# A decoder layer in split fp32: order of loads, casts and products at four places, and who makes the low parts

## The chip, the core and the metric

The kernel runs on one core of one Trainium2 chip. The metric is the device time of one execution in microseconds (us), median of several runs. The engines are PE (TensorE), DVE (VectorE), ACT (ScalarE), POOL (GpSimd) and SP, whose queue issues nearly all transfers.

## The reference, cut to what matters

One decoder layer on x (1024 tokens, width 1024, fp32), with 256 memory tokens. Three sub-layers, each with an RMS norm ahead and a residual behind:

```python
h = rms_norm(x, norm_mix)
rq, rk, rv, rg, dq, dk, dv = split(h @ w_in)
o_ret  = rms_norm(retention(rotary(rq), rotary(rk), rv)) * silu(rg)
o_diff = rms_norm(diff_attention(norm(dq), norm(dk), dv, lam), diff_subln) * 0.8
x = x + (concat(o_ret, o_diff) * group_scale) @ w_out
k, v = split(rms_norm(mem, norm_mem) @ xkv);  q = norm(rms_norm(x, norm_x) @ xq)
x = x + softmax(q @ norm(k).T / 16) @ v @ xo
h = rms_norm(x, norm_ffn)
x = x + (silu(h @ w_gate) * (h @ w_up)) @ w_down
```

Retention has 8 heads of 64 in chunks of 128 tokens, differential attention 4 heads, cross-attention 4 heads of 256; the FFN is 2816 wide.

## The kernel before, in words

**Split products.** Each fp32 operand of a large product is held as a high part (a cast to fp32r, mostly on ACT) and a low part (the rest, a subtract in `low`, L104, on DVE or POOL). `mm3` (L134) issues three matmuls for each block: high by high, high by low, low by high. `unit` (L121) loads one 128 x 1024 block of a weight into a staging buffer (`raw`, three buffers; some into `t4`, six), casts it and makes its low part on the engine named by `eng`.

**Who sets the order.** PE's instructions keep the order of the program. Those of the other engines and the transfers are ordered at compile time by a scheduler, by program position and by when it expects operands and buffers; `tc.high_priority()` moves a block ahead of it, and `keep_in_program_order` pins single ones. A tile waits for a free buffer of its pool: PSUM has two buffers each of `mm`, `ms` and the two-bank `s2`.

**Start.** `xT` is x transposed, in four pairs (q) of 256 tokens and two halves (j). `load_xT` (L219) loads one and, except for q = 0, multiplies it by the norm's gain on POOL in four pieces; `split_x` (L234) casts and subtracts it; for q = 0 the gain is in both. `token_norm` takes the squares of the token rows on ACT and their inverse roots on DVE. The loop over n (L739) then runs 64 items, eight token blocks of each of eight heads: `gemm` (projection, four items ahead, in four parts), `e1` and `e3` (norm and transpose of keys), `m1`, `m2`, `m3` (scores, transposes, values).

**Memory stage.** The last items run beside `Mem.gemm` (L632): keys and values of the memory tokens for eight column blocks c, 24 matmuls for each of two token blocks t. `Mem.load` loads the two weight units of block c + 2. The finished heads lie in DRAM as `mix_d`; `load_mix` (L693), called at the end of block c, loads one head's rows into a `raw` buffer, and casts and splits it. Four of the six `t4` buffers hold the memory tokens in this stage. The output projection (L827) follows, its four weight units a column half; each token block's norm and transposes (`to_hT`, kept as closures in `mend`) run behind, the last four of them after the projection.

**Cross-attention.** Items n = 4 h + p, head h, token pair p: `xG` query product, `xR` inverse norms, `xS` scores, `xT_` transposes of the weights, `xO` values, `xX` (L997) output product in four parts (two token blocks, two column halves), each added to the residual `xr` on DVE. For the last head, `xX` also takes the FFN's norm of the pair: square on ACT, inverse root and scale on DVE into a tile `xn_f` (two buffers), then `b_sums` (L847) makes four differences of its quarters.

**Border to the FFN.** The FFN's first products use seven forms (1 to 7) of the normed input, a recursion that saves one product in eight. `b_part(p, f)` (L870) transposes form f of pair p on PE, casts the high part on ACT and makes the low part: for pair 0 on DVE; for others a product with minus the identity (`negI`) subtracts the high part in PSUM and ACT casts the rest, one `b_part` later (`b_flush`). `Forms` makes the forms of a weight pair, and `GU` (L1154) runs the products; the first weight is done in two halves, `c0` (pairs 0 and 1) and `c1` (pairs 2 and 3).

**End.** The down projection sums 11 pairs of hidden blocks for each of seven forms (L1332); for the last form the last three pairs are held back and done one output block i after the other, so that `d_out` adds and stores each as it is finished.

## Time and profile before

| | |
|---|---|
| runs of before | 1631.23, 1631.32, 1632.48 us; median 1631.32 |
| the profiled execution's own time | 1633.47 us |
| its span, first to last instruction | 1631.7 us |
| busy share: PE, DVE, ACT, POOL | 95%, 61%, 38%, 19% |
| mean granted clock of PE | 0.985 |
| chain that ended last, by engine | PE 76%, DVE 13%, ACT 4%, DMA 3%, POOL 2% |

The span is that of one profiled execution. Busy time counts an engine's instructions; PE's are pipelined, so that a busy PE need not be at its peak. "Idle before" is time an engine stood before an instruction, with what released it. PEclk is the clock granted to PE, 1.00 being 2.4 GHz and 0.50 being 1.2 GHz. An engine that is not the bottleneck may idle at no cost.

### The profile page before, as it was taken

What the parts mean: (1) busy time and instruction counts of PE and PEld (TensorE: products, weight loads), DVE (VectorE), ACT (ScalarE), POOL (GpSimd) and SP (SyncE); (2) the same over time, 40 slices, a digit from 0 to 9 for tenths busy, and PEclk for the clock granted to TensorE, in tenths of its full rate; (3) what the DMA queues carried; (4) which work ended last, traced back from release to release, by engine and by line L of the source; (5) the groups of instructions that cost most, each with busy time, mean ns of one, the idle gap of its engine ahead of it and who ended that gap; (6) DMA issues with size and microseconds to landing.
All of it is one profiled execution on the core that took longest, in us unless ns stands there. A gap on an engine that the chain in (4) does not pass through costs nothing.

```text
span 1631.7 us, 23450 instructions
## 1 busy us (share of the span) xinstructions
PE 1555.4 (95%) x8797; PEld 1328.1 (81%) x8797; DVE 995.0 (61%) x2494; ACT 626.9 (38%) x1209; POOL 310.8 (19%) x428
## 2 busy tenths in 40 slices
PE   6899999999999889999999979999999999999998
PEld 6778888878888878799999867887888888788886
DVE  6954864964866633755555855666666666555554
ACT  5442443442445531332233454333333333343332
POOL 5423323323303432111112220000000000000000
PEclk9899999999999999999999999999999999999999
DMA  8201011111103552100101222444444444788562
GB/s 287 72 27 50 34 40 40 44 40 39 40 14 134 188 182 91 40 13 29 39 27 39 78 91 67 165 149 148 149 148 149 161 149 162 256 302 260 202 211 78
DMA packets 69233, 180.85 MB, mean 111 GB/s; under 512 B 7424, under 2 KB 12928, under 8 KB 69120
## 3 DMA queue, kind: packets, MB, share of 16 engines
q1 hardware_dynamic: 68112, 178.81, 31.1%
q8 instruction: 69, 1.13, 0.3%
q10 hardware_dynamic: 1008, 0.55, 0.1%
q14 instruction: 44, 0.36, 0.1%
HBM read 135.55 MB, written 43.78 MB: 110 GB/s over the span
## 4 chain that ended last, share of the span: by engine, by line
PE 76%; DVE 13%; ACT 4%; DMA 3%; POOL 2%; issue 1%; SPq 0%; ACTq 0%; DVEq 0%; POOLq 0%
PE x L64 15%; PE g_r L64 8%; PE z L64 7%; PE dx L64 7%; PE dy L64 6%; PE xq L64 5%; PE wo L64 5%; PE xo L64 5%; PE y L64 3%; PE kv L64 3%; PE q L64 2%; PE av L64 2%; DVE nmx L52 2%; DVE dsm L52 1%; PE rsk L64 1%
## 5 line engine op out<-in xcount | busy, mean ns | idle before, releaser
L64 PE MATMUL g_r<-uh_r,xT 128*128 128x512 f32 x512 | 179.3, 408 | 0.0
L52 DVE TENSOR_TENSOR dl<-ds,dh 128x1024 fp32r<-128x1024 f32 x77 | 93.9, 1223 | 93.2 <-PE dx L64 37.4
L52 ACT CAST dh<-ds 128x1024 fp32r<-128x1024 f32 x77 | 80.7, 1055 | 123.8 <-PE dy L64 49.9
L64 PEld LDWEIGHTS g_r<-uh_r,xT 128*128 128x128 f32 x512 | 97.1, 190 | 22.5 <-issue 2.4
L64 PE MATMUL x<-Bh,f 128*128 128x512 f32 (+1 forms) x368 | 113.3, 380 | 1.4 <-DVE G L52 1.4
L52 POOL TENSOR_TENSOR G<-G,U 128x512 f32<-128x512 f32 (+1 forms) x23 | 35.3, 1537 | 408.5 <-DVE U L52 347.5
L64 PE MATMUL kv<-uh_d,xT 128*128 128x256 f32 x512 | 109.6, 297 | 1.2 <-DVE dql L52 1.2
L52 DVE TENSOR_TENSOR f<-s,f 128x512 fp32r<-128x512 f32 x86 | 65.4, 761 | 62.2 <-ACT f L52 62.2
L64 PE MATMUL g_r<-ul_r,xT 128*128 128x512 f32 x256 | 101.1, 395 | 0.0
L52 ACT CAST f<-s 128x512 fp32r<-128x512 f32 x88 | 54.6, 621 | 106.2 <-DVE s L52 105.7
L64 PE MATMUL xq<-hT,uh_xq 128*128 128x256 f32 x512 | 94.3, 286 | 0.0
L64 PE MATMUL xo<-uh_xo,xoT 128*128 128x512 f32 x256 | 89.4, 409 | 3.6 <-DVE xr L52 2.0
L64 PEld LDWEIGHTS kv<-uh_d,xT 128*128 128x128 f32 x512 | 86.0, 195 | 3.7 <-DVE dql L52 1.4
L52 ACT ACTIVATE p<-s,nmx,dsm 128x128 f32<-128x128 f32 (+7 forms) x64 | 53.2, 832 | 87.0 <-DVE nmx L52 86.2
L64 PEld LDWEIGHTS xq<-hT,uh_xq 128*128 128x128 f32 x512 | 80.5, 193 | 0.0
L64 PEld LDWEIGHTS x<-Bh,f 128*128 128x128 f32 x368 | 68.3, 188 | 14.9 <-DVE G L52 1.8
L52 DVE TENSOR_TENSOR G<-x,G 128x512 f32<-128x512 f32 (+1 forms) x69 | 45.6, 661 | 50.2 <-ACT G L52 47.8
L64 PE MATMUL kv<-ul_d,xT 128*128 128x256 f32 x256 | 73.5, 287 | 1.0 <-DVE ul_d L52 1.0
L64 PE MATMUL xq<-hT,ul_xq 128*128 128x256 f32 x256 | 73.1, 286 | 0.0
L52 DVE TENSOR_TENSOR f<-gu,f 128x512 fp32r<-128x512 f32 x61 | 42.0, 689 | 49.6 <-ACT f L52 49.6
L64 PE MATMUL dx<-dh 128*128 128x512 f32 x176 | 68.8, 391 | 1.6 <-DVE res L52 1.6
L64 PE MATMUL x<-Bl,f 128*128 128x512 f32 (+1 forms) x184 | 69.9, 380 | 0.0
(337 smaller groups left out, 4257.0 us busy)
## 6 DMA issues: line engine op xcount, KB each, us to landing
gu<-in_w_dram SPq DMA_DIRECT2D x21, 1024.0 KB, 6.0
ds<-gF_d SPq DMA_DIRECT2D x77, 256.0 KB, 4.0
wd<-in_w_dram SPq DMA_DIRECT2D x22, 512.0 KB, 5.6
wT_d<-wd SPq DMA_DIRECT2D x22, 512.0 KB, 3.0
ds<-wT_d SPq DMA_DIRECT2D x44, 256.0 KB, 4.0
ds<-in_w_dram SPq DMA_DIRECT2D x33, 256.0 KB, 5.1
st_r<-in_w_dram SPq DMA_DIRECT2D x16, 512.0 KB, 3.2
st_kv<-in_w_dram SPq DMA_DIRECT2D x16, 512.0 KB, 3.4
```

Of the source, the lines that this page charges most:

```text
L52: r = f(*args, **kw)
L64: return tc.keep_in_program_order(nc.tensor.matmul(*args, **kw))
```

## The change

Start: pair q = 1 of `xT` takes its gain in `split_x`, like q = 0, and no longer on POOL; the scores of item 0 (`m1`) are issued behind the third quarter of the next projection. Memory stage: all low parts of its weights go to DVE; `load_mix` is called at the start of block c with a `t4` buffer, and the new `split_mix` casts at the end of c; in the output projection units 0 and 2 have DVE for the low part and 1 and 3 POOL, the reverse of before. Cross-attention: the first query product `xG(0)` is issued ahead of the four last transposes rather than after the first of them. Border: `b_sums` of pair 1 goes to POOL, in pieces of 256 columns; low parts of pairs 0 and 1, and of forms 2, 5, 7 and 4 of the others, go to DVE; only items 14 and 15 have high priority in `xX`; the transposes, values and output products of item 15 are issued earlier, and the `b_part` calls of pairs 1 to 3 are spread between the FFN's first products. End: two pairs are held back, not three.

```diff
--- before.py
+++ after.py
@@ -1,4 +1,4 @@
-from contextlib import ExitStack
+from contextlib import ExitStack, nullcontext
 
 import numpy as np
 
@@ -221,7 +221,7 @@
         st = stage(f"xs{q}_{j}")
         xst[q, j] = st.rearrange("p (k t) -> p k t", k=4)
         sp.dma_start(xst[q, j], a["xT"][:, 4 * j:4 * j + 4, 256 * q:256 * q + 256])
-        if q:
+        if q > 1:
             g = bc(gains[:, G_MIX + 4 * j:G_MIX + 4 * j + 4], 256)
             for i in range(4):
                 tc.keep_in_program_order(gp.tensor_tensor(out=xst[q, j][:, i:i + 1], in0=xst[q, j][:, i:i + 1],
@@ -235,7 +235,7 @@
 
         s3 = xst.pop((q, j))
         hv, o = xT[q // 2], 256 * (q % 2)
-        if q:
+        if q > 1:
             hi, lo = (hv[:, 4 * j:4 * j + 4, x, o:o + 256] for x in range(2))
             sc.copy(hi, s3)
             low(ve, lo, s3, hi)
@@ -629,12 +629,13 @@
 
         def load(self, c):
             if c < 8:
-                self.u[c] = [unit(U_KV + 2 * c + i, f"kv{c}_{i}", eng=ve if i else gp, pool=up if i else uqp, pin=c < 1) for i in range(2)]
+                self.u[c] = [unit(U_KV + 2 * c + i, f"kv{c}_{i}", eng=ve, pool=up if i else uqp, pin=c < 1) for i in range(2)]
 
         def gemm(self, c, i):
             t, h = divmod(i, 2)
             if i == 0:
                 self.load(c + 2)
+                load_mix(c)
             if h == 0:
                 self.ps = mm(f"xkv_{c}_{t}")
             ps = self.ps
@@ -650,7 +651,7 @@
                 sc.activation(sq, dst, AF.Square, accum_out=self.ssk[:, 4 * t + c:4 * t + c + 1])
             if t == 0:
                 return
-            load_mix(c)
+            split_mix()
             if c == 3:
                 rsqrt(self.ssk, 8, 1.0 / 256, "kx")
                 for j in range(2):
@@ -690,16 +691,22 @@
 
     kord = [g + (4 if kind == "d" else 0) for kind, g in order]
 
+    mixs = []
+
     def load_mix(i):
-        if i >= len(kord) - 1:
-            return
-        kb = kord[i]
-        st = raw(f"mixs{kb}")
-        sp.dma_start(st, mix_d[kb])
-        for h in range(2):
-            sl = slice(512 * h, 512 * h + 512)
-            sc.copy(mixT[h][:, kb, 0, :], st[:, sl])
-            low(ve, mixT[h][:, kb, 1, :], st[:, sl], mixT[h][:, kb, 0, :])
+        if i < len(kord) - 1:
+            kb = kord[i]
+            st = t4(f"mixs{kb}")
+            sp.dma_start(st, mix_d[kb])
+            mixs.append((kb, st))
+
+    def split_mix():
+        if mixs:
+            kb, st = mixs.pop(0)
+            for h in range(2):
+                sl = slice(512 * h, 512 * h + 512)
+                sc.copy(mixT[h][:, kb, 0, :], st[:, sl])
+                low(ve, mixT[h][:, kb, 1, :], st[:, sl], mixT[h][:, kb, 0, :])
 
     def run_fin(last=False):
         if fins:
@@ -754,7 +761,6 @@
         if n == 0:
             call("e3", 0)
             call("e3", 1)
-            call("m1", n)
             split_x(3, 1)
             call("e1", 3)
             token_norm(3)
@@ -763,6 +769,8 @@
             ws[1] = [load_part(*order[1], i) for i in range(4)]
         drain(pend2)
         gemm(n + LEAD, (2,))
+        if n == 0:
+            call("m1", n)
         run_fin()
         gemm(n + LEAD, (3,))
         drain(pend3)
@@ -825,7 +833,7 @@
             dst[t // 4] = big.tile([P, KB, 2, 512], F32R, tag="A", name=f"{name}{t // 4}")
 
     for c in range(2):
-        u = [unit(U_OUT + 4 * c + i, f"wo{c}_{i}", eng=ve if i % 2 else gp, pool=ntp if c and i < 2 else None)
+        u = [unit(U_OUT + 4 * c + i, f"wo{c}_{i}", eng=gp if i % 2 else ve, pool=ntp if c and i < 2 else None)
              for i in range(4)]
         for t in range(NT):
             ps = mm(f"wo_{c}_{t}")
@@ -848,12 +856,13 @@
 
         ev, od = xns
         xns.clear()
-        eng = gp if p < 1 else ve
+        eng = gp if p < 2 else ve
         T1, T2, T4 = (hfp.tile([P, 512], F32, tag=f"bs{i}", bufs=1, name=f"bs{p}_{i}") for i in (1, 2, 4))
         T3 = od[:, 0:512]
         for dst, l, r in ((T1, od[:, 0:512], ev[:, 0:512]), (T2, od[:, 512:1024], T1), (T4, ev[:, 512:1024], T2),
                           (T3, od[:, 512:1024], od[:, 0:512])):
-            eng.tensor_tensor(out=dst, in0=l, in1=r, op=ALU.subtract)
+            for c in cut4(512) if eng is gp else (slice(0, 512),):
+                eng.tensor_tensor(out=dst[:, c], in0=l[:, c], in1=r[:, c], op=ALU.subtract)
         bsrc[p] = {1: ev[:, 0:512], 2: ev[:, 512:1024], 3: od[:, 512:1024], 5: T1, 6: T2, 7: T3, 4: T4}
 
     def b_tiles(f):
@@ -876,7 +885,7 @@
         lo, hi = (x[:, :, P * p:P * p + P] for x in b_tiles(f))
         sc.copy(hi, p3)
         b_flush()
-        if p == 0:
+        if p < 2 or f in (2, 5, 7, 4):
             low(ve, lo, p3, hi)
             return
 
@@ -1004,14 +1013,15 @@
                       cols(uo[i:i + 1], 0, 1024, 512 * c, 512)) for i in range(2)])
 
             sl = xr[t][:, 512 * c:512 * c + 512]
-            ve.scalar_tensor_tensor(out=sl, in0=ps, scalar=Z[:, e:e + 1], in1=sl, op0=ALU.mult, op1=ALU.add)
+            with tc.high_priority() if n > 13 else nullcontext():
+                ve.scalar_tensor_tensor(out=sl, in0=ps, scalar=Z[:, e:e + 1], in1=sl, op0=ALU.mult, op1=ALU.add)
             if h == 3 and c == 1:
                 sp.dma_start(res_d[t], xr[t])
                 if e == 0:
                     hd["r"] = small(2, "rn2", f"rf{p}")
                 xn = xnp_tile(f"xn_f{t}")
                 xns.append(xn)
-                with tc.high_priority():
+                with tc.high_priority() if n > 13 else nullcontext():
                     r = hd["r"]
                     sc.activation(xn, xr[t], AF.Square, accum_out=r[:, e:e + 1])
                     if p == 3:
@@ -1024,8 +1034,8 @@
                     if e:
                         b_sums(p)
 
+    xG(0)
     mend.pop(0)(mm)
-    xG(0)
     mend.pop(0)(mm)
     head_k(0)
     mend.pop(0)(mm)
@@ -1055,16 +1065,18 @@
     xS(15)
     b_part(0, 5, ms)
     xX(14, (0, 1))
-    b_part(0, 6, mm)
+    b_part(0, 6, ms)
+    with tc.high_priority():
+        xT_(15)
+    xX(14, (2, 3))
     b_part(0, 4, ms)
-    xX(14, (2, 3))
-    for i, f in enumerate((1, 2, 3)):
-        b_part(1, f, (mm, ms)[i % 2])
-    xT_(15)
-    for i, f in enumerate((5, 6, 7, 4)):
-        b_part(1, f, (mm, ms)[i % 2])
-    xO(15)
+    with tc.high_priority():
+        xO(15)
+    b_part(1, 1, ms)
+    b_part(1, 2, ms)
+    xX(15, (0, 1))
     b_flush()
+    xX(15, (2, 3))
 
 
 
@@ -1222,26 +1234,29 @@
     f0.form(1, gp)
     f0.form(2, gp)
     o = GU(0, f0)
+    def b_parts(p, *fs):
+        for f in fs:
+            nb[0] += 1
+            b_part(p, f, (ms, ms, mm)[nb[0] % 3])
+
+    nb = [0]
+    for f, eng in ((5, gp), (6, ve), (3, gp), (7, ve), (4, gp)):
+        f0.form(f, eng)
     o.go(1, c0)
+    b_parts(1, 3, 5)
     o.go(2, c0)
-    for f, eng in ((5, gp), (6, ve), (3, gp)):
-        f0.form(f, eng)
-    xX(15, (0, 1), ms)
-    xX(15, (2, 3), ms)
-    f0.form(7, ve)
-    f0.form(4, gp)
+    b_parts(1, 6, 7)
     o.go(5, c0)
+    b_parts(1, 4)
     o.prod(6, c0)
-    for i, f in enumerate((1, 2, 3)):
-        b_part(2, f, (mm, ms)[i % 2])
+    b_parts(2, 1, 2)
     o.go(3, c0)
-    for i, f in enumerate((5, 6, 7)):
-        b_part(2, f, (ms, mm)[i % 2])
+    b_parts(2, 3, 5)
     o.go(7, c0)
-    b_part(2, 4, mm)
+    b_parts(2, 6, 7)
     o.go(4, c0)
-    for i, f in enumerate((1, 2, 3, 5, 6, 7, 4)):
-        b_part(3, f, (ms, mm)[i % 2])
+    b_parts(2, 4)
+    b_parts(3, 1, 2, 3, 5, 6, 7, 4)
     fn = Forms(1)
     o.go(1, c1)
     b_flush()
@@ -1341,12 +1356,12 @@
             if (f, p) not in du:
                 d_load(f, p, raw if p % 2 else t4)
                 d_cast(f, p)
-            if f != d_order[-1] or p < NP - 3:
+            if f != d_order[-1] or p < NP - 2:
                 for i in range(4):
                     d_prod(f, p, i)
         if f == d_order[-1]:
             for i in range(4):
-                for p in range(NP - 3, NP):
+                for p in range(NP - 2, NP):
                     d_prod(f, p, i)
                 d_out(f, i)
         else:
```

## Rows read from the trace of the kernel before

**Rows 1.** Windows by stage: us, busy PE, PEld, DVE, ACT, POOL; PEclk, DMA, GB/s.

```profile
17.00:60.00 43.00, 31.60 (x212) 29.53 (x211) 37.80 (x174) 26.48 (x56) 29.09 (x41) 0.80 0.56 198
...
500.00:592.00 92.00, 79.20 (x553) 72.14 (x551) 53.62 (x108) 49.02 (x96) 44.17 (x55) 0.93 0.51 181
...
730.00:900.00 170.00, 169.53 (x1176) 157.58 (x1176) 94.74 (x254) 51.51 (x105) 36.91 (x51) 1.00 0.11 38
...
930.00:970.00 40.00, 31.24 (x177) 24.94 (x175) 28.76 (x67) 21.59 (x43) 9.14 (x10) 0.96 0.29 113
970.00:1013.00 43.00, 37.37 (x229) 31.97 (x230) 19.73 (x45) 23.25 (x46) 1.91 (x3) 0.96 0.08 25
```

**Rows 2.** Windows of two of the stretches at half clock, columns as above.

```profile
43.45:53.69 10.24, 6.90 (x33) 6.47 (x33) 10.21 (x58) 3.75 (x8) 5.58 (x8) 0.50 0.30 110
...
685.16:688.57 3.41, 3.41 (x18) 3.41 (x18) 3.10 (x12) 0.86 (x2) 1.28 (x1) 0.50 0.35 129
```

**Rows 3.** Waits of PE over the span: waiting, releaser, us in total, times, longest.

```profile
PE xkv L64 <- ACT vx L52: 7.6, 3, 4.0
...
PE s L64 <- DVE dkT L52: 4.7, 1, 4.7
PE q L64 <- ACT dkv L52: 3.7, 1, 3.7
...
PE tr_x L68 <- DVE xr L52: 2.7, 1, 2.7
```

**Rows 4.** Timeline of the start, engines ACT, POOL and DVE: start, us, what.

```profile
10.02 1.71 ACT L52 ACTIVATE xT<-xs,gains 128x256 fp32r<-128x256 f32 x4 [1.31 <-DMA xs<-in_xT_dram]
...
23.18 1.04 ACT L52 ACTIVATE x<-x 128x1024 f32<-128x1024 f32 x1
...
14.29 12.40 POOL L52 TENSOR_TENSOR xs<-xs,gains 128x256 f32<-128x256 f32 x16 [13.23 <-DMA xs<-in_xT_dram]
...
24.34 0.17 DVE L52 TENSOR_SCALAR rx_x<-rstd 128x2 f32<-128x2 f32 x1 [0.41 <-ACT x L52]
...
47.01 0.34 DVE L52 SCALAR_TENSOR_TENSOR dkT<-dkt,gx,dkT 128x128 fp32r<-128x128 f32 x1
```

**Rows 5.** Groups by form, 500 to 592 us: busy us, mean ns, idle before.

```profile
L52 POOL TENSOR_TENSOR ul_kv<-st_kv,uh_kv 128x256 fp32r<-128x256 f32 x32 | 28.8, 933 | 34.4 <-ACT uh_kv L52 34.4
...
L52 ACT CAST uh_kv<-st_kv 128x1024 fp32r<-128x1024 f32 x16 | 16.5, 1046 | 15.7 <-DMA st_kv<-in_w_dram 15.4 <-PE xkv L64 0.3
...
L52 DVE TENSOR_TENSOR ul_kv<-st_kv,uh_kv 128x1024 fp32r<-128x1024 f32 x8 | 10.3, 1290 | 10.5 <-ACT uh_kv L52 10.4
...
L52 ACT CAST mix<-mixs 128x512 fp32r<-128x512 f32 x14 | 8.1, 620 | 12.1 <-DMA mixs<-mix_d 12.1
```

**Rows 6.** Chain of waits, 500 to 592 us: start, us, what.

```profile
535.70 2.79 PE xkv L64 x24
...
576.66 3.27 DMA mixs<-mix_d
```

**Rows 7.** Windows of two parts of the border, columns as in the first group.

```profile
936.60:942.00 5.40, 1.78 (x8) 1.10 (x7) 5.40 (x9) 0.00 (x0) 0.00 (x0) 1.00 0.09 37
942.00:951.00 9.00, 6.79 (x40) 4.78 (x41) 2.31 (x9) 8.36 (x18) 0.00 (x0) 1.00 0.15 60
```

**Rows 8.** Groups by form, 930 to 1000 us, of ACT and DVE.

```profile
L52 DVE SCALAR_TENSOR_TENSOR xn_f<-xr,rf,g_ffn 128x1024 f32<-128x1024 f32 x6 | 7.5, 1283 | 0.3
...
L52 ACT ACTIVATE xn_f<-xr 128x1024 f32<-128x1024 f32 x4 | 4.3, 1086 | 0.0
L52 DVE TENSOR_TENSOR bs<-xn_f,bs 128x512 f32<-128x512 f32 x6 | 4.1, 684 | 0.0
```

**Rows 9.** Timeline of DVE around the start of a POOL subtract at 507.05.

```profile
506.88 0.16 DVE L52 TENSOR_TENSOR rw_m<-ry_m 128x2 f32<-128x2 f32 x1
...
507.85 0.67 DVE L52 SCALAR_TENSOR_TENSOR ry_m<-rw_m,ry_m 128x2 f32<-128x2 f32 x1
```

**Rows 10.** Chain of waits at the end of the kernel.

```profile
1624.60 0.70 DVE res L52
```

## The prediction

> **What bounds the kernel now.** The page's first part shows TensorE (PE) busy for 95% of the span and VectorE (DVE), the next, for 61%. So I asked for the busy time of each engine in stretches and looked where PE's share falls. In most of the kernel it idles for under 3%; the exceptions [rows 1] are four: 11.4 us of idle in the start, 12.8 us in the stage that multiplies the memory tokens while heads finish, and 8.8 + 5.6 us in the border from cross-attention to the FFN. The fourth is one wait at the border into cross-attention, below. In the same places the granted clock is 0.50, that is 1.2 instead of 2.4 GHz [rows 2]: after an idle of 2 to 5 us PE works at half speed for 3.41, 6.83 or 10.24 us. Besides the two stretches shown, the places that the change touches hold two of 6.83 us, at 23.0 and 558.9, and four of 3.41: at 514.5 and 582.8 (memory stage), 961.6 and 971.9 (border). The PE time inside such a stretch is lost by half. All else in the kernel is PE at work, which the change barely touches. So the question is who ends each wait: the list of PE's waits names them [rows 3], and I read each in the timeline of the engine named.
>
> **Start (17 to 60 us).** PE waits 3.7 us for the copy `dkv`, and that copy stood on ScalarE (ACT) behind the cast of the second token pair and behind two squares of `x`, the second from 23.18 to 24.22 [rows 4]; the cast waited for 8 gain multiplies on GpSimd (POOL). Then PE waits 4.7 us for DVE's last `dkT` part, at 47.01; from 24.34 on DVE is never idle, so that end is set by when DVE could begin. The change gives the gains of that pair to the cast, as for the first: 8 ACT pieces (four took 1.71 us) and 8 DVE pieces of about 0.5 us instead of two of 1.2 to 1.7 us: about +0.5 us for DVE. The first half of the pair has landed when POOL takes it up, at 14.29 [rows 4]; with the second half close behind and 3.4 us of ACT pieces the cast can end near 18 to 19, the squares near 20, where the second now ends at 24.22. DVE begins 3 to 4 us sooner; later pairs' loads do not move, so I take 3. Moving the scores of block 0 behind the next 12 products fills 1.4 us of the second wait (24 took 2.79 us [rows 6]; double that at half clock). **Sum: -4.5.** Bounds: 0, if the later loads set DVE's chain, and -8, two thirds of the idle and of the half-speed loss.
>
> **Memory stage (500 to 592 us).** The chain of waits runs in a ring: a low part on POOL (32 pieces, 28.8 us), a load into the staging buffer that it frees, a cast, PE [rows 5, 6]. ACT stands 15.4 us for weight loads and 12.1 us for `mixs` loads, and PE's next product waits for the evacuation `vx` queued behind such a cast. The change breaks the ring in three places. The `mix` rows get their own buffer and are issued one step ahead of the cast, while PE has 48 products, 5.6 us, against a load of 3.27; this moves seven DMAs on SP's queue past the cast and returns the third staging buffer to the weights. Eight low parts go from POOL, four pieces of 0.93 us each, to DVE, 1.29 us each: DVE +10.3, to 64 of 92 us. And the output weights that are used first get the faster engine. To be won: 12.8 of idle and half of about 11.7 us of work at 1.2 GHz, 18.7 together. I leave 8: 2.1 at the heads' own waits (511 to 523), some 2 of the 4 us at 557 where ACT stands behind a reduce of DVE, 1.7 for one half-speed stretch, 2.2 at the first output weights and elsewhere. **Sum: -10.5.** Bounds: -4, if the new buffer (six, four of them held by the memory tokens) gives no lead and only POOL's part counts, and -15.
>
> **Into cross-attention (681 us).** The transposes need the PSUM buffer whose reader `xr` stands in DVE's queue behind a norm: 2.7 us, then 3.41 us at 0.50, which costs 1.7 [rows 2, 3]. The query product now goes first: 48 products, 5.6 us, inputs ready, so the reader is covered. But two transposes now follow each other on two PSUM buffers, each waiting for a cast and a subtract (1.3 us); I give back 1.4. **Sum: -3**, bounds 0 and -4.4.
>
> **Border (930 to 1013 us).** Two views tell the halves apart [rows 7]. From 936.6 to 942 DVE is busy throughout (norms and sums of the second pair, put first) while PE works 1.8 of 5.4 us; from 942 to 951 ACT is full, casting high and low parts, while DVE stands idle for three quarters. The change: (a) 15 low parts leave PE and ACT for DVE: 15 products of 512 columns less on PE, at 0.23 us twice those of 256 [rows 6], 3.5; ACT -9; DVE +10.3 at 0.68, the time of a sum of that size [rows 8]; (b) the sums of pair 1 go to POOL, DVE -2.7, with work between them and their first use; (c) products stand between the transposes. To be won: 14.4 idle, 3.4 of half speed, 3.5 of products: 21.3. Put back: the norm of a pair needs the two `xn_f` buffers, whose last readers, transposes 3 and 7, now come late. Pair 2: a square of 1.09, some 13 small DVE operations of 0.2 each, a scale of 1.28 [rows 8, 9] are 5.1 us from transpose 7 of pair 1, against 3.6 us of products and a transpose group: 1.5. Pair 3 the same with ten small operations: 4.6 against 3.4, 1.2, and its four sums of 0.68 chained with low parts on one engine, 2. Behind the last attention output 0.7. DVE's added 7.6 us (10.3 - 2.7) come where it is busy 58% of the time: I take 3.6 on the path. Two half-speed stretches stay, 3.4. Together 12.4. **Sum: -9.** Bounds: -2 and -15.
>
> **Last pairs.** Holding two pairs back instead of three leaves the count of products and the last add and store as they are; the waits for that add (0.70 us, [rows 10]) stay, one for each buffer of two banks. 0, bounds +0.8 and -0.8. Later scale operations without priority (first two pairs) are covered: they fall where PE is busy nearly throughout, as in the 169.5 of 170 us before them [rows 1].
>
> **Sum.** -4.5 - 10.5 - 3 - 9 = -27. The profiled execution took 1633.47 us (span 1631.7 and 1.8 around it), 2.15 over the median of the three runs, 1631.32. So 1606.5 by its own time, 1604.4 by the median; I say **1605**.
>
> **Rivals.** (1) *The waits change hands.* Order in the program is not the order of readiness: if PE next waits for DVE at the start, for the casts' pool in the memory stage and for the late `xn_f` buffers in the border, with the half-speed stretches staying, I take 2 + 5 + 1 + 3 = 11: 1620. For it: DVE is already unbroken from 24.3 to 47. Against: in the two larger places the engine that takes the work is the idle one [rows 1, 7].
>
> (2) *POOL's sums hold DVE.* A small DVE operation takes 0.16 us alone and 0.67 beside a POOL subtract [rows 9]. The sums of pair 1 and the low parts of the first FFN weights on POOL now fall beside the two norm chains: 9 of 13 operations at +0.5 us make 4.5 each, 9 for two: the border's gain is gone, 1614. Against: POOL's 8 pieces are early, and by the same rows DVE gains where low parts leave POOL. The Trainium skill, "SBUF — State Buffer", section "SBUF: two separate sides", has it that a GpSimd operation and a DVE operation with two SBUF inputs lock each other out for a whole instruction; the 0.67 us agree, a POOL piece being about that long. By that rule alone the memory stage speaks for this change and the border against it.
>
> (3) *DVE becomes the bound; slower.* Memory stage +10.3, border +7.6, start +0.5 of DVE work, 18.4, all on PE's path with no wait gone, less 3 + 1.4 for products that fill waits: +14, 1645. It decides once the low parts delay PE by more than the removed waits, above all if DVE in the memory stage comes near 80 of 92 us; it would have 64. So it is unlikely.
>
> (4) *No change*: loads and casts were ordered so already, or gains and losses cancel: 1631.
>
> **Chances.** Forecast 0.58, (1) 0.20, (2) 0.12, (3) 0.06, (4) 0.04. The forecast's own bounds, not all met at once, give 1595 to 1614; up to 1621 the range takes in (1) and (2) and leaves out under 0.2. By the 0.2% (3.3 us) that a measurement of this kernel can tell: faster 0.90, the same 0.04, slower 0.06.
>
> **What would show it.** Start: no PE wait for `dkv`, the first square on ACT before 19, the first scores near 42 to 43. Memory stage: no POOL `ul_kv`, ACT without waits for `mixs`, `vx` waits under 3 us, PE idle in it under 6 us. Cross-attention: `xq` right behind `wo`, no wait of 2 us. Border: 15 `negI` products fewer (6 left), ACT and DVE near balance, a PE wait of 1 to 2 us before transpose 1 of pair 2 and 3 of pair 3. End: unchanged from the last hold on. Wrong would be: DVE busy over 75 us in the memory stage, a PE wait for `ul_kv` there, or waits for `xn_f` over 5 us each.

## The result and the profile after

The changed kernel takes 1603.07 us (median of four runs, 1601.9 to 1604.63) where the kernel before, run beside it, takes 1631.28: ratio 0.9829, 95% interval 0.9812 to 0.9846. The forecast was 1605, in a range of 1595 to 1621. The profiled execution took 1601.9 us, its span is 1600.1; PE is busy for 96% of it, DVE for 63%, ACT for 39%, POOL for 18%, and the granted clock is 0.994 on average.

The windows by stage of the changed kernel (columns as in [rows 1]: start of the window, length, then the busy time of PE, its weight loads, DVE, ACT and POOL, granted clock, DMA share, GB/s):

```profile
17.00:58.00 41.00, 29.96 (x222) 27.71 (x221) 40.09 (x181) 25.23 (x56) 23.32 (x35) 0.88 0.60 211
...
492.00:571.00 79.00, 78.08 (x578) 71.73 (x578) 60.45 (x130) 52.25 (x101) 19.70 (x23) 1.00 0.66 223
...
659.00:704.00 45.00, 40.94 (x317) 38.80 (x316) 27.18 (x82) 15.81 (x35) 2.77 (x2) 1.00 0.05 16
...
905.00:942.00 37.00, 29.60 (x188) 26.24 (x188) 32.52 (x74) 17.60 (x36) 11.61 (x14) 0.96 0.26 100
942.00:980.00 38.00, 31.80 (x201) 27.27 (x200) 24.04 (x51) 19.91 (x40) 4.55 (x6) 0.95 0.14 54
```

Against [rows 1], the memory stage has turned from 12.8 us of idle at a clock of 0.93 into a stretch where PE works 78.08 of 79 us at full clock, with POOL's share halved. The start, the way into cross-attention and the border still idle. The list of PE's waits in the changed kernel says for whom (waiting, releaser, us in total, times, longest):

```profile
PE bt L64 <- DVE xn_f L52: 5.2, 2, 3.1
PE dss L64 <- DVE dkT L52: 4.3, 1, 4.3
PE tr_x L68 <- DVE hT L52: 3.6, 2, 3.2
PE dkt L68 <- DVE dkv L52: 3.0, 1, 3.0
...
PE xot L64 <- DVE B6l L52: 2.1, 1, 2.1
```

Of the waits in [rows 3] none is left under its name: the 7.6 us for `vx` are gone altogether; the waits for `dkv` on ACT, `dkT` and `xr` have successors, every one of them now on DVE.

To say where the 31.6 us between the two profiled spans came from, I take the start of the same product of PE in both traces: the first of `q`, the first of `g_r` (second head), the last of `wo`, the 25th of `xs` (third scores of cross-attention), the 181st of `xs` (sixteenth scores), the 49th of `z` (FFN under way). In brackets, PE's time at granted clock 0.50 in that stretch, all us:

| kernel | start: `q` to `g_r` | heads and memory: to last `wo` | into cross-attention: to 25th `xs` | border: 181st `xs` to 49th `z` | 49th `z` to the end of the last product |
|---|---|---|---|---|---|
| before | 65.97 (17.07) | 606.81 (20.48) | 42.64 (3.41) | 78.29 (6.83) | 620.03 |
| after | 63.12 (10.24) | 586.28 (3.41) | 41.51 (0) | 71.61 (6.83) | 619.94 |
| difference | -2.85 | -20.53 | -1.13 | -6.68 | -0.09 |

The second column also holds 6.83 us at half clock in before (at 183.4 and 432.6) and 3.41 in after (at 304.0), in heads that the change does not touch. PE is busy all through these three stretches, so half of them is lost; without that the column reads 603.40 and 584.57, **-18.8**, and that is the memory stage. From the third to the sixteenth scores, between the third column and the fourth, both kernels take the same time (206.39 and 206.46).

In the three other places PE stands idle almost as long as before. Start, way into cross-attention and border by the same milestones, first three windows of the kernel before, then three of the changed one (columns as above):

```profile
7.56:73.53 65.97, 52.77 (x363) 48.85 (x363) 58.52 (x243) 36.85 (x85) 35.83 (x49) 0.87 0.53 188
680.34:722.98 42.64, 38.78 (x286) 36.71 (x285) 26.64 (x75) 14.64 (x31) 4.76 (x5) 0.96 0.07 26
929.38:1007.67 78.29, 63.90 (x387) 53.17 (x386) 45.09 (x110) 42.47 (x85) 11.05 (x12) 0.96 0.20 74
```

```profile
7.58:70.70 63.12, 50.29 (x363) 46.40 (x363) 60.90 (x249) 38.26 (x91) 27.34 (x41) 0.92 0.55 196
656.97:698.49 41.52, 37.46 (x287) 35.27 (x286) 26.72 (x75) 14.95 (x31) 4.80 (x5) 1.00 0.08 26
904.95:976.55 71.60, 58.00 (x372) 50.73 (x371) 54.37 (x121) 35.17 (x70) 16.16 (x20) 0.95 0.21 81
```

The idle time, length less busy PE, is 13.2 and 12.8 us in the start, 3.9 and 4.1 ahead of cross-attention, 14.4 and 13.6 in the border. What became shorter is the time in which PE works: in the first two places it works less at half clock, in the border it has 15 products fewer.

Three views of the changed kernel carry this reading. First the timeline of the start (ACT, then POOL, then DVE: start, us, what):

```profile
17.12 1.05 ACT L52 ACTIVATE x<-x 128x1024 f32<-128x1024 f32 x1
...
19.36 4.76 POOL L52 TENSOR_TENSOR xs<-xs,gains 128x256 f32<-128x256 f32 x8 [18.30 <-DVE xT L52]
...
19.73 0.41 DVE L52 TENSOR_SCALAR rx_x<-rstd 128x2 f32<-128x2 f32 x1
...
23.03 0.54 DVE L52 SCALAR_TENSOR_TENSOR ry_x<-rw_x,ry_x 128x2 f32<-128x2 f32 x1
...
24.18 0.16 DVE L52 TENSOR_TENSOR rw_x<-rw_x,rx_x 128x2 f32<-128x2 f32 x1
...
43.08 0.34 DVE L52 SCALAR_TENSOR_TENSOR dkT<-dkt,gx,dkT 128x128 fp32r<-128x128 f32 x1
```

Against [rows 4] the squares end before 20 and the norm begins at 19.73 instead of 24.34, as forecast. But POOL's multiplies for the third pair now fall beside it, and until they end at 24.12 eight of its small operations take 0.41 to 0.54 us instead of some 0.16; in the kernel before four did. The last `dkT` part comes 3.9 us sooner, not 4.6.

Second, ACT's waits in the memory stage of the changed kernel, to be set beside the idle times in [rows 5]:

```profile
ACT mix L52 <- DMA mixs<-mix_d: 3.8, 1, 3.8
...
ACT uh_kv L52 <- DMA st_kv<-in_w_dram: 2.8, 5, 0.8
```

15.4 us for weights have become 2.8, and 12.1 for the `mix` rows 3.8. Third, DVE on the way into cross-attention:

```profile
662.46 1.09 DVE L52 SCALAR_TENSOR_TENSOR rw_x<-ry_x,rx_x 128x1 f32<-128x1 f32 x1
...
664.68 1.28 DVE L52 SCALAR_TENSOR_TENSOR xn_x<-xr,r_x,g_x 128x1024 f32<-128x1024 f32 x1
665.88 0.68 DVE L52 TENSOR_TENSOR xqT<-xq,xqT 128x512 fp32r<-128x512 f32 x1
666.48 1.28 DVE L52 TENSOR_TENSOR hT<-tr_x,hT 128x512 fp32r<-128x512 f32 x2
```

PE's first two transpose groups ended at 663.99; their low parts `hT` stand in DVE's queue behind the whole norm of token block 7 and behind `xqT`, until 666.48. The 1.09 us of the norm's small operation fall beside a POOL piece of 1.28 us, from 662.26 on (`xv`).

### The profile page after: what moved, and what is told of

The parts are those of the page before. It is cut to its first block, busy times and chain, and to the rows that moved or that the text cites. A ratio compares the mean times of both kernels' runs of the same rounds, so it can differ in the third digit from the quotient of the medians.

```text
span 1600.1 us, 23423 instructions
## 1 busy us (share of the span) xinstructions
PE 1537.4 (96%) x8782; PEld 1315.1 (82%) x8782; DVE 1008.9 (63%) x2519; ACT 621.0 (39%) x1200; POOL 282.4 (18%) x400
## 3 DMA queue, kind: packets, MB, share of 16 engines
q8 instruction: 69, 1.13, 0.3%
## 4 chain that ended last, share of the span: by engine, by line
PE 78%; DVE 15%; ACT 3%; DMA 2%; issue 2%; POOL 0%; ACTq 0%; SPq 0%; DVEq 0%; POOLq 0%
PE x L64 15%; PE g_r L64 9%; PE z L64 8%; PE dx L64 7%; PE dy L64 6%; PE xo L64 5%; PE wo L64 5%; PE xq L64 5%; PE y L64 3%; PE kv L64 2%; PE xkv L64 2%; PE av L64 2%; PE q L64 2%; DVE nmx L52 2%; DVE dsm L52 1%
```

## The experiments

Twelve kernels, each read by the same milestones. The first four are the kernel before with edits of the memory stage, all three or one.

**The memory stage, part by part.** All three edits, whose diffs follow one by one:

> The kernel before with the three edits of the memory stage alone (mix rows loaded one step ahead into buffers of their own, the even low parts of the key/value weights on DVE, the engines of the output weights' low parts exchanged). In the whole change this stage went 18.5 us shorter, by the start of the same products. Theory (the stage's gain is its own): -17 to -19, about 1613. Rival (part of it came from the shorter start, or the places of half-speed stretches): -12 or less, 1619 or more. Left untouched: start, cross-attention, border within 1 us.

Only the rows of `mix` loaded ahead, and from `t4`:

```diff
+                load_mix(c)
...
-            load_mix(c)
+            split_mix()
...
-        st = raw(f"mixs{kb}")
+            st = t4(f"mixs{kb}")
```

> The kernel before with only the mix rows' loads moved one step ahead and into the other buffers. Theory (ring: staging buffer, load, cast, PE; POOL's low parts are one link, the mix rows the other): ACT loses its 12.1 us of waits for mixs, POOL still holds the weights' buffers; -8 to -12 us, about 1621. Rival 1 (the mix loads were the whole of it): -16 to -18. Rival 2 (POOL's low parts are the whole of it): -3 or less.

Only the low parts of the key/value weights on DVE:

```diff
-                self.u[c] = [unit(..., eng=ve if i else gp, ...
+                self.u[c] = [unit(..., eng=ve, ...
```

> The kernel before with only the even low parts of the key/value weights on DVE instead of POOL. Theory (ring): staging buffers come free sooner, but ACT still stands behind the mix loads: -4 to -8, about 1625. Rival 2 (POOL's low parts are the whole of it): -15 or more, 1616 or less. Third possibility (DVE becomes late for the evacuations): +1 or more.

Only the engines of the output weights exchanged:

```diff
-        u = [unit(U_OUT + ..., eng=ve if i % 2 else gp, ...
+        u = [unit(U_OUT + ..., eng=gp if i % 2 else ve, ...
```

> The kernel before with only the engines of the output weights' low parts exchanged. Theory: PE's wait at the first output products is bound by the weight load as much as by the low part, so -1 to -2, 1629.5 to 1630.5. Rival (the stage's end is set there): -4 or more.

| kernel | whole, ratio to before | `g_r` to last `wo` | less half of the half-clock time before 490 | against before |
|---|---|---|---|---|
| all three | 0.987 (0.9855 to 0.9884) | 588.73 | 585.32 | -18.1 |
| loads ahead alone | 1.000 (0.9986 to 1.0014) | 610.98 | 609.27 | +5.9 |
| low parts alone | 0.9912 (0.989 to 0.9934) | 594.75 | 593.04 | -10.4 |
| exchange alone | 0.9978 (0.9966 to 0.9989) | 604.21 | 604.21 | +0.8 |

Each row of the last three columns is one profiled execution; that of the loads ahead was the slowest of its ten (1636.35 us, median 1633.23).

The stage's gain is its own: -18.1 with nothing else changed. Of the places left untouched, start and way into cross-attention stayed within 1 us, as expected; the border came out 2.9 shorter, with no half-clock stretch where before has 6.83 us. But it is not three links that each pay. The loads ahead alone gain nothing, where -8 to -12 was expected. PE's waits in that run, from 492 to 600:

```profile
PE xkv L64 <- POOL ul_kv L52: 5.0, 2, 4.7
PE xkv L64 <- ACT vx L52: 4.8, 2, 4.3
```

With the `mix` loads out of the way PE waits for POOL's low parts themselves, which [rows 3] don't list; the wait has a new name and the stage is no shorter. Why it is 5.9 longer, the rows leave open. With the low parts on DVE instead, which gains more than the 4 to 8 expected, the products run through, and a single long wait is left, at the first output weights:

```profile
PE wo L64 <- ACT uh_wo L52: 5.0, 1, 5.0
```

with 10.24 us at half clock from 572.5 on. So POOL's low parts were the first link and decide; the loads ahead come second and pay only behind them. The exchange alone shows how easily a run misleads: its whole is 0.2% faster by an interval that excludes no change, but in the profiled execution its stage is not shorter. There the half-clock stretches at 183 and 432 are missing, and the one ahead of cross-attention, and that is 5.1 us.

**Two parts undone at a time**, in places far apart. First the loads ahead, and the sums of pair 1:

```diff
-        eng = gp if p < 2 else ve
+        eng = gp if p < 1 else ve
...
-            split_mix()
+            load_mix(c)
```

> The changed kernel with two parts undone in places 350 us apart: the mix rows are again loaded right ahead of their casts into the staging buffers (memory stage), and the sums of pair 1 are again on DVE (border). Memory stage: by the first four runs the low parts on DVE gave 13 and the exchange of engines 4 of 21, so the mix loads are worth the rest once POOL is out of the way: +3 to +5, as a wait for the first output weights with a half-speed stretch behind it. Rival (loads ahead are worth nothing beside the other two): within 0.7 of the changed kernel. Border: DVE is busy 32.5 of 37 us there and gets 2.7 more: +1 to +3. Rival (POOL's sums hold DVE, rival 2 of the prediction): -1 to -3, with DVE's two-input operations back at 0.68 where they took 1.03 to 1.23.

Whole 0.9891 (0.9874 to 0.9907). Memory: 593.99, less 1.71 for one stretch, 592.28, 7.7 over the changed kernel and more than the 3 to 5 expected; the wait is the expected one, at the first output weights:

```profile
PE wo L64 <- ACT uh_wo L52: 3.6, 1, 3.6
```

So the loads ahead, worth nothing alone, are worth 7 to 8 us here (the runs with all three and with all but these differ by 592.28 - 585.32 = 7.0). Border: 72.75 against 71.61, as expected in size, but with 17.07 us at half clock instead of 6.83. PE worked in 13.5 and 6.83 of them; half of the difference, an estimate of its cost, is 3.3. Without it the border would be some 2 us shorter than that of the changed kernel, as rival 2 had it. DVE's sums of the first FFN weights, beside no POOL sums, take 0.68 us again where they took up to 1.23; rival 2 has its mechanism, and its price is not settled by this run.

Then the gains of the second pair, and the border's low parts:

```diff
-        if q > 1:
+        if q:
...
-        if p < 2 or f in (2, 5, 7, 4):
+        if p == 0:
```

> The changed kernel with two parts undone 880 us apart: the gains of the second token pair are again on POOL (start), and the 20 low parts of pairs 1 to 3 that the change gave to DVE are PE's and ACT's again (border). Start: theory (the gains held the squares and the norm): +2.5 to +3.5, the first square on ACT back near 22, with PE's wait for dkv; rival (the products ahead of block 0's scores gave it): within 0.7. Border: theory (ACT is the bound from 942 on): +3 to +6, ACT full again; rival (the border's gain is the interleaved order alone, and the low parts on DVE cost what they save): within 1, or shorter.

Start: 69.11, 6.0 over the changed kernel where 2.5 to 3.5 was expected, and the second square on ACT is back at 23.18. PE worked 16.4 us at half clock here and 5.7 in the changed kernel, which by half is 5.4 of the 6.0. The products ahead of block 0's scores do not give the gain. Border (15 low parts moved back, not 20): **69.09, 2.5 shorter than the changed kernel**, some 2.0 of it one half-clock stretch less (PE worked 2.9 and 6.83 us in them), where +3 to +6 was expected. The border by windows, beside the last line of the changed kernel's above:

```profile
914.49:983.58 69.09, 60.87 (x388) 52.08 (x387) 43.41 (x106) 42.34 (x85) 16.85 (x20) 0.98 0.22 84
```

PE has more products, works 2.9 us longer, and stands idle for 8.2 us instead of 13.6. The `negI` products fill time in which PE otherwise stood waiting, mostly for DVE's norm; a low part on DVE stands in the same queue as that norm. The low parts moved to DVE cost the border at least what they saved, as the rival had it. What it gained is left to its other edits, the interleaved order above all; no run takes order and priorities apart.

**Orders and buffers.** Next, the two late-buffer theories of the prediction at once:

```diff
     mend.pop(0)(mm)
-    mend.pop(0)(mm)
+    mend.pop(0)(ms)
...
+    b_part(1, 3, ms)
     xX(15, (0, 1))
+    b_part(1, 7, ms)
...
-    b_parts(2, 3, 5)
+    b_parts(2, 3, 7, 5)
```

> The changed kernel with two orders altered. Into cross-attention, the second of two transposes that follow each other takes the other pair of PSUM buffers: if the 3.23 us of wait there are the two shared buffers, as the prediction said, at most 0.5 stays, -2.5 to -3; if DVE's queue ahead of it (a norm's scale of 1.28) is the cause, the wait moves to the next transposes and -1 or less is gained. Border: transposes 3 and 7 of each pair, the last readers of the norm's buffers, stand ahead of 5, 6 and 4: if the waits of 2.08, 1.17 and 3.09 us are these late buffers, -4 to -6 (with the two half-speed stretches up to -8); if DVE's amount of work is the cause, within 1.5. Whole: about 1596.

Whole 0.9869 (0.9854 to 0.9883). Neither shortened its stretch. Into cross-attention the wait moved one place on, as the second case had it:

```profile
PE xkt L68 <- DVE hT L52: 3.6, 1, 3.6
```

and with 10.24 us at half clock the stretch takes 46.16. Two more PSUM buffers for one transpose do not take the wait away; DVE's queue is late. Border 71.68 against 71.61: the waits for `xn_f` shrink from 5.2 us to 1.8, but PE now waits 1.5 for `G` and 0.8 each for `B4l` and `B6l`, all on DVE. In all it stands idle for 10.8 us instead of 13.6, so the late buffers were part of the cause; but half clock doubles to 13.65, PE working in 12.1 of them, and by half that is 2.6, about what the shorter waits won.

As that run, with the gains of the third pair on the cast as well and the low parts of the next FFN weights on DVE:

```diff
-        if q > 1:
+        if q > 2:
...
-    fn.form(1, gp)
-    fn.form(2, gp)
+    fn.form(1, ve)
+    fn.form(2, ve)
```

> As the run before, and two more edits. Start: the gains of the third token pair go to the cast as well, so that no POOL multiply runs beside the first norm (its small operations took 0.54 us beside them and 0.16 after): -1 to -2 at the first scores; if DVE's 16 added pieces of about 0.5 us weigh more, +1 to +2. Border: the two low parts of the next FFN weights go from POOL to DVE, so that the norm of token 6 is not beside them (four operations of 0.66 instead of 0.16): -1 to -2; if DVE is full there, +0.5 to +1. Whole: about 1593.

Whole 0.9861 (0.9846 to 0.9876). Start 62.76, against 63.12 in the changed kernel, 64.06 and 64.68 in the two other runs with its start: -0.4 to -1.9. Border 71.42, 0.3 shorter: the four slow norm operations were not what it waited for.

Then one edit in each place:

```diff
-        if q > 1:
+        if q > 2:
...
+            call("m1", n)
...
-    xG(0)
-    mend.pop(0)(mm)
-    mend.pop(0)(mm)
-    head_k(0)
+    mend.pop(0)(ms)
+    xG(0)
+    mend.pop(0)(mm)
+    head_k(0)
...
-        if p < 2 or f in (2, 5, 7, 4):
+        if p == 0:
...
-    b_part(0, 6, ms)
+    with tc.high_priority():
+        b_part(0, 6, ms)
...
-    b_part(0, 4, ms)
+    with tc.high_priority():
+        b_part(0, 4, ms)
```

> The changed kernel with one edit in each place that the runs so far left open. Cross-attention: the first transposes go ahead of the query product again, but into the PSUM buffers whose reader is a plain low part; the product then covers DVE's queue before the second. If DVE's queue behind the norm is the cause of the 3.23 us, as the last runs say, no wait over 1 us is left from the last output product to the third scores: 41.5 to about 38.5. Rival (the first transposes now wait, for xn or for those buffers): 41 or more. Border: low parts of pairs 1 to 3 on PE and ACT (they were 2.5 shorter there), and the casts and low parts of products 6 and 4 of pair 0 ahead in the queues, for the wait of 2.06 on B6l: from 69.1 of that run to 66 or 67; if DVE then delays xr and xn_f instead, 69 again. Start: gains of the third pair on the cast, scores of block 0 not moved behind the 12 products: if the move costs when the squares are early, the first product of the second head comes 1 to 2 sooner than 70.5; if it pays, 1 to 2 later. Whole: about 1596.

and the same with block 0's scores behind the 12 products, the order of the border from above, and two products in the scores' buffers:

```diff
-            call("m1", n)
...
+    def sb(name):
+        return s2(name)[:, 0:512]
...
-    b_part(1, 1, ms)
-    b_part(1, 2, ms)
+    b_part(1, 1, sb)
+    b_part(1, 2, sb)
+    b_part(1, 3, ms)
     xX(15, (0, 1))
+    b_part(1, 7, ms)
```

> As the run before with two differences. Start: the scores of block 0 behind the 12 products, as in the change: 70.5 for the first product of the second head. Border: products 3 and 7 of each pair ahead of 5, 6 and 4, and products 1 and 2 of pair 1 in the PSUM buffers of the scores: if the late norm buffers still set the end, another -2 to -3, 64 to 65; if ACT, which has the low parts now, sets it, within 1. Whole: about 1595.

Whole 0.9812 (0.979 to 0.9834) and 0.985 (0.9821 to 0.9878). Into cross-attention 42.94 and 42.80, a miss: a wait of 2.4 for `hT` stays, with 6.83 at half clock. Border 71.46 and 77.02, both misses: half clock 3.41 and 13.65; no run takes the second apart. Start 62.74 without the moved scores, 63.69 with them, but 10.24 and 17.07 us of them at half clock: what the move is worth stays open. The first run's DVE and POOL showed what the way into cross-attention waits for:

```profile
653.18 0.66 DVE L52 SCALAR_TENSOR_TENSOR ry_x<-rw_x,ry_x 128x1 f32<-128x1 f32 x1
...
656.74 1.72 DVE L52 SCALAR_TENSOR_TENSOR xn_x<-xr,r_x,g_x 128x1024 f32<-128x1024 f32 x1
658.38 0.68 DVE L52 TENSOR_TENSOR xr<-wo,xres 128x512 f32<-128x512 f32 x1
...
652.39 6.67 POOL L52 TENSOR_TENSOR ul_xo<-st_xo,uh_xo 128x256 fp32r<-128x256 f32 x8 [38.15 <-ACT hT L52]
```

While POOL makes the low parts of the first head's output weights, needed some 30 us later, the norm of block 6 runs at 0.66 us an operation and its scale at 1.72 instead of 1.28. Behind it the last `xr` is late, so the norm of block 7, so the `hT` parts that PE waits for; the next run tests this chain.

**The queue on DVE.** POOL's pieces taken away there, and the border's low parts divided:

```diff
-        uo = [unit(U_XO + 2 * h + i, f"xo{h}_{i}") for i in range(2)]
+        e = gp if h else ve
+        uo = [unit(U_XO + 2 * h + i, f"xo{h}_{i}", eng=e) for i in range(2)]
...
-        low(gp, vh[:, :, 1, :], vsl, vh[:, :, 0, :])
+        low(e, vh[:, :, 1, :], vsl, vh[:, :, 0, :])
...
-        if p < 2 or f in (2, 5, 7, 4):
+        if p < 2:
```

> The changed kernel with three edits. Cross-attention: the low parts of the first head's output weights and of its values go from POOL to DVE. In the run with the products in another order, eight POOL pieces (652.4 to 659.1) stood beside the norm of token block 6, whose small operations took 0.66 us instead of 0.16 to 0.22, and the norm of block 7 began late for it; the low parts of the transposes queue behind that norm. If POOL's pieces are the cause, the wait of 3.23 us behind the first transposes falls to 0.5 to 1.5, and from the last output product to the third scores 41.5 becomes 39 to 40. Rival (DVE's added 3.3 us stand ahead of the norm just as long): 41 or more. Border: pairs 0 and 1 keep their low parts on DVE, pairs 2 and 3 have theirs on PE and ACT: the 2.6 us for B5l of pair 1 behind ACT's square go, and the second half, where all of ACT's low parts gave 47.8 and DVE's 50.2, comes at 46 to 47; border 67 to 68 by the same products. Rival (the half-speed stretches fall otherwise): 71. Start: gains of the third pair on the cast and the scores behind the products: 0.9 under the changed kernel, within the spread of 1. Whole: 1595 to 1598.

Whole 0.9815 (0.9794 to 0.9836). Into cross-attention 40.33, the wait down from 3.23 to 2.05; border 68.28. The chain of the same norm, now with no POOL beside it:

```profile
656.30 0.16 DVE L52 SCALAR_TENSOR_TENSOR ry_x<-rw_x,ry_x 128x1 f32<-128x1 f32 x1
656.49 0.22 DVE L52 SCALAR_TENSOR_TENSOR rw_x<-ry_x,rx_x 128x1 f32<-128x1 f32 x1
...
657.37 1.22 DVE L52 TENSOR_TENSOR ul_xo<-st_xo,uh_xo 128x1024 fp32r<-128x1024 f32 x1
658.52 1.28 DVE L52 SCALAR_TENSOR_TENSOR xn_x<-xr,r_x,g_x 128x1024 f32<-128x1024 f32 x1
```

The operations are fast again, and two low parts of 1.22 take much of the time so won: a gain of 1.2, 0.3 short of what was expected.

Last, the PSUM buffers shared out otherwise:

```diff
+    def sb(name):
+        return s2(name)[:, 0:512]
...
     xG(0)
     mend.pop(0)(mm)
-    mend.pop(0)(mm)
     head_k(0)
+    mend.pop(0)()
     mend.pop(0)(mm)
...
-    b_part(0, 6, ms)
+    b_part(0, 6, sb)
...
-    b_part(0, 4, ms)
+    b_part(0, 4, sb)
```

> The run before with PSUM buffers shared out otherwise. Border: products 6 and 4 of pair 0 go into the scores' PSUM buffers, so that the last attention output no longer waits for DVE's B6l: the 2.06 us go (-1.5 to -2.1 in the first half, 21.4 to 19.5); rival: the wait only moves to the next late operation of DVE, xr or Bl, and 21 stays. Cross-attention: after the query product one transpose group in the two product buffers, the key transposes, and one in a scores buffer, so PE has 2.7 us of work before it needs a buffer again instead of 2.06 (with the rest in the same queue): 40.3 to 39.3 to 39.8; rival (xqT, squares and scores start later for it): 40.5 or more. Second half of the border: 46.9 as before. Whole: 1594 to 1597.

**1595.15 us, ratio 0.9772 (0.9753 to 0.9791), faster than both kernels**; the interval lies clear of the changed kernel's. Against the run before, the first half of the border (181st `xs` to the first product of the FFN) takes 19.55 for 21.43, the whole border 66.97 for 68.28, the way into cross-attention 38.38 for 40.33, a microsecond better than expected. PE's waits from 650 to 990:

```profile
PE bt L64 <- DVE xn_f L52: 2.3, 2, 2.1
PE bt L64 <- DVE xoT L52: 1.3, 1, 1.3
PE xo L64 <- DVE xr L52: 1.3, 1, 1.3
...
PE tr_x L68 <- DVE hT L52: 0.7, 1, 0.7
```

The 2.06 us for `B6l` are gone, and the waits for `xoT` and `xr` beside it, 1.0 and 1.1 in the changed kernel, grew by half a microsecond. A free scores buffer did what a higher priority on DVE had not (first half 22.37). Ahead of cross-attention PSUM buffers do count, once the norm is faster: PE's longest wait there fell from 2.0 to 0.7 us.

## Why the prediction was right, and where it was not

The sum was right by two errors that cancel: the memory stage gave 8 us more than forecast, the three other places together 5.8 less.

- **Start, -4.5 forecast, -2.85 measured** (-1.2 to -2.8 for the three runs with its start against 65.87, the median of the five with before's). Right: the gains on the cast, the squares before 20, DVE 4.6 us sooner, no wait for ACT's `dkv`. Mis-sized: both terms, since the waits changed hands. A wait of 3.0 for `dkv` on DVE came in place of the 3.65 on ACT. "Moving the scores of block 0 behind the next 12 products fills 1.4 us of the second wait" did not hold either: the wait went to the product that now comes first, `dss`, 4.3 us that the profile puts down to `dkT` again. PE's idle fell by 0.4 us. What went is the half-clock stretch of 6.83 us at 23.0; the one of 10.24 stayed. Not seen: four more small operations of the norm at about 0.5 us beside POOL's later multiplies.
- **Memory stage, -10.5 forecast with a bound of -15, -18.8 measured.** The mechanism was right, the size failed at one step: "I leave 8". Each of the four remainders was a piece of the same delay. Once POOL's low parts were out and the `mix` rows came ahead, the heads' waits, the wait behind the reduce, the half-clock stretch and the wait at the output weights were gone; the whole of "18.7 to be won" came. "Breaks the ring in three places" misled too: one link decides, the second pays 7 only behind it, the third shows no gain alone. DVE, forecast at 64 of 92 us, was busy 60.45 of 79 and no bound (rival 3).
- **Into cross-attention, -3 forecast, -1.13 measured, and that largely by luck.** The product did cover the reader `xr`. But PE's idle did not fall (3.9 and 4.1 us); the gain comes from the missing half-clock stretch, which does not stay away: the two runs with parts undone have the same code here, 3.41 and 10.24 us at half clock, and take 42.32 and 45.50, before 42.64. The step that failed is "each waiting for a cast and a subtract (1.3 us); I give back 1.4": 3.23 us came back, since the subtract stood behind a norm in DVE's queue. Two more PSUM buffers for one transpose did not help; a faster norm took 1.2 us off, and other PSUM buffers behind it another 2.0.
- **Border, -9 forecast, -6.68 measured.** The sum let PE's idle fall by 5.4 us (14.4 won; 1.5, 3.2, 0.7 and 3.6 put back) and took 3.5 for the products. The products gave more: PE works 5.9 us less, with 6.83 us at half clock in both kernels. The idle gave 0.8. The waits named were there, at twice their size: before pair 2 2.08 and 1.17 for 1.5, in pair 3 0.86, 1.32, 0.34 and 3.09 for 3.2, around the last attention output 2.06 and 0.97 for 0.7. Late buffers are part of their cause, half-clock time hides what earlier readers won. The step that failed is the price of (a), 15 low parts more on DVE, "I take 3.6 on the path": undoing it took 5.4 us of PE's idle away, more than the products it brought back, and made the border 2.5 shorter, half-clock time apart about 0.5.
- **Last pairs, 0 forecast, -0.09 measured** up to the end of the last product.
- **Rivals.** Rival 1 came true in three places of four: waits changed hands in the start, ahead of cross-attention and in the border, but not in the memory stage, which holds most of the gain. POOL did hold DVE's operations, in three places. Where it was taken away, cross-attention gained 1.2 us, the start 0.4 by the medians of four runs (62.76 to 63.81) and three (63.12 to 64.68), which is within their spread, and the border 0.3 with the weights' low parts and an estimated 2 with the sums, far under the 9 of rival 2.
- **Signs and slips.** Four signs failed: PE still waits for `dkv`, now on DVE; ACT waits once for `mixs` (3.8 us); PE waits over 2 us ahead of cross-attention (3.23); ACT and DVE are not near balance in the border (35.2 and 54.4 us busy). The start's terms, 3 and 1.4, make 4.4, without the 0.5 us added to DVE. The border's norms, as listed, make 5.0 and 4.4 us and not 5.1 and 4.6. Ahead of the half-clock stretches of before, PE's idles were 1.0 to 4.7 us and not "2 to 5". None of these decides the sum.

Of the 31.6 us between the two profiled spans, 1.7 are half-clock stretches elsewhere. The medians differ by 28.2, since the profiled execution of before lay above its median and that of after below.

## What to carry to other kernels

When a wait is one turn of a ring (buffer, load, cast, product), find the link that holds the others before you price them one by one: take it away alone, and expect small waits around it to go with it, while repairs to later links show nothing until then. Before work goes to an engine with idle time, look at what stands in its queue at that moment: here a low part on DVE beside a norm cost PE at least as much as the same part on PE and ACT. And compare stages by the start of the same product, with PE's idle time and its time at half clock noted apart: three of the four places became shorter with hardly less idle, and an edit that did nothing in its place came out 0.2% faster.

## What the runs showed that was not expected of the hardware

- DVE operations with two inputs in SBUF slow down beside POOL, those that read PSUM do not: beside the same eight POOL pieces the scale of the norm took 1.72 us (1.28 alone) and its small operations 0.66 (0.16), while `xr`, whose input is PSUM, took 0.68 as everywhere. At the start, operations with one SBUF input were slowed too (`TENSOR_SCALAR` of 128x2, 0.54 for 0.17). The Trainium skill, "SBUF — State Buffer", section "SBUF: two separate sides", has a lock between a GpSimd operation and a DVE operation with two SBUF inputs; the trace agrees.
- Time at the granted clock of 0.50 differs widely for the same products: the border had none in the run with the memory stage alone (75.39 us) and 6.83 in the kernel before (78.29), with the same code there; over all runs it had 0 to 17.07. Differences of 3 us between kernels mean little until these stretches are counted.
